# A recurrence's level products: three fp16 matmuls of split operands, or one fp32 matmul

## The chip, the core and the metric

One core of one Trainium2 chip runs the whole program. The metric is the device time of one execution in microseconds (us); the kernel before took 3277.73 us (median of 3 runs, 3277.06 to 3282.74). A core has five engines that run side by side, each taking its own instructions in order: TensorE (PE; its weight loads are listed as PEld), VectorE (DVE), ScalarE (ACT), GpSimd (POOL) and SyncE (SP), which issues DMAs.

## What is computed

Two transformer blocks over 2048 tokens of width 1024. The change lies in the second, in its recurrence (HGRN2), four heads of 128 channels each over 16 meta tokens and 2048 tokens:

```
def hgrn2(q, f_raw, i, lb):
    # f = lb + (1-lb) sigmoid(f_raw), S_t = diag(f_t) S_{t-1} + (1-f_t) i_t^T, o_t = S_t^T q_t
    ...
    diff = bcum[:, :, :, None, :] - bcum[:, :, None, :, :]
    decay = jnp.exp(jnp.where(tri[:, :, None], diff, -jnp.inf))
    scores = jnp.sum(qc[:, :, :, None, :] * decay * kc[:, :, None, :, :], axis=-1)
    o_intra = jnp.einsum('bhts,bhsv->bhtv', scores, vc)
    new_state = (jnp.exp(b_last[:, :, 0, :])[..., None] * state
                 + jnp.einsum('bhsk,bhsv->bhkv', kc * jnp.exp(b_last - bcum), vc))
    return new_state, o_inter + o_intra
```

The same block has a sparse attention of 8 heads (a latent of 128, 256 selected keys), then a gated output projection and a layer norm.

## The kernel before, in words

The program runs in phases: projections and attention of the first block, projections of the second, a selection of keys, and then `phase_dsa`, in which three things are woven together: the second block's attention (4 groups of 512 queries times 8 heads, 32 steps), the output projection (`out2`, `norm2`), and the recurrence (`Hgrn`, the class at line 1811).

An attention step computes scores in `pst` (lines 2101 to 2113), takes their exponential on ScalarE (line 747), splits it in two fp16 parts `phi` (ScalarE, line 749) and `plo` (mostly GpSimd, line 753), and multiplies by the values with three fp16 matmuls (lines 777 to 779). Beside it the next head's score maxima are found: a matmul into `p` (line 2052) and a masked maximum on VectorE (line 2058), collected in `mu`, written by line 764 to 766 into `zrow`, and turned by a matmul (line 769).

`Hgrn.chunk(t)` (line 1870) works off 256 tokens, t = 0 to 7, as eight blocks (four heads, two halves of 128 tokens). A block's 128 by 128 matrix of decayed scores `Ts` is built by seven levels m = 1, 2, 4 ... 64: at a level, the queries in the upper half of each group of 2m tokens meet the keys of its lower half. `kq` (fp32, k in its first half, q in its second) holds keys and queries with the decay up to the group's border multiplied in. A level does this:

- ScalarE casts the needed columns of `kq` to fp16, `Xh` (line 1911); what is lost is `Xl`, a subtraction (line 1912), on GpSimd at levels 0, 2 and 4 (`XP`), on VectorE at the others. Both have two buffers (`XB`).
- TensorE makes eight products of 64 columns into `pl`, each from three fp16 matmuls: high by high, high by low, low by high (lines 1917 to 1919).
- VectorE copies `pl` under a mask into `Ts` (line 1924; line 1921 at m = 64).
- `double` (line 1838) multiplies, in place, the decay of the other half group into `kq`: k on GpSimd (`UP`), q on VectorE (line 1846), and joins two decays in `dc` (line 1847).

After the levels, `Ts` and the state give the output `o` in fp32 matmuls (lines 1935 and 1936), `update` moves the state on (lines 1855 to 1867), and the rows are normalised (lines 1942 to 1953). Line 1899 (eight fp32 matmuls with a moving operand of one column) makes the diagonal.

The order on each engine is not written by hand: the builder emits attention steps and fills them with chunks and projection tiles at given places (`CH`, `O2`), each with a priority (`PC`, `PO`), and a scheduler puts every engine's instructions in order by its own costs before the program runs. In the trace, chunk 0 to 7 lie between 2270 and 3070 us of the span. A second copy of `phase_dsa` stands in a branch that these inputs don't take.

Of the kernel before, what the change touches and what calls it, by code (L numbers as in the profile page):

```python
# [13 lines left out]
F16 = mybir.dt.float16  # L14
# [3 lines left out]
ALU = mybir.AluOpType  # L18
# [16 lines left out]
LATE = -800  # L35

KSC = 2.0 ** 14
XP = (0, 2, 4)
FB, XB, OT = 1, 2, "o"
UP = (0, 1, 2, 3, 4, 5, 6)  # L40
UQ = ()

# [44 lines left out]
def ap(t, off, pat):  # L87
    return bass.AP(tensor=t.tensor, offset=t.offset + off, ap=[list(p) for p in pat])
# [1722 lines left out]
class Hgrn:  # L1811
# [58 lines left out]
    def chunk(self, t):  # L1870

        K, sp, lp = self.K, self.sp, self.lp
        nc = K.nc
# [31 lines left out]
        d, o = fT.rearrange("p h t -> p (h t)"), 0  # L1905
        for li, m in enumerate(LEVELS):

            X = ap(kq, 0, [list(kq.ap[0]), [2 * m, 512 // m], [1024 + m, 2], [1, m]])
            hi, lo = (sp.tile([128, 8, 128], F16, name=n, bufs=XB) for n in ("Xh", "Xl"))
            h3, l3 = (x.rearrange("p h (n a m) -> p (h n) a m", a=2, m=m) for x in (hi, lo))  # L1910
            nc.scalar.copy(h3, X)
            (nc.gpsimd if li in XP else nc.vector).tensor_tensor(l3, X, h3, op=ALU.subtract)
            p = self.py.tile([128, 8, 64], F32, name="pl", tag="y")
            M = 64 if m == 64 else 128
            for h in range(8):
                qv = [x[:, h].rearrange("p (n a m) -> p n a m", a=2, m=m)[:, :, 1] for x in (hi, lo)]
                nc.tensor.matmul(p[:M, h], lhsT=hi[:, h, :M], rhs=qv[0], start=True, stop=False)
                nc.tensor.matmul(p[:M, h], lhsT=hi[:, h, :M], rhs=qv[1], start=False, stop=False)
                nc.tensor.matmul(p[:M, h], lhsT=lo[:, h, :M], rhs=qv[0], start=False, stop=True)
            if m == 64:  # L1920
                nc.vector.tensor_copy(Ts[:64, :, 64:], p[:64])
            else:
                d4 = lambda x: x.rearrange("p h (n m) -> p h n m", m=m)
                nc.vector.copy_predicated(Ts.rearrange("p h (n a m) -> p h n a m", a=2, m=m)[:, :, :, 1],
                                          d4(self.mk[:, li, None, :].to_broadcast([128, 8, 64])), d4(p))
            dn = dt[:, o:o + 512 // m]
            self.double(kq, d, dn, m, 2, li)
            d, o = dn, o + 512 // m
# [403 lines left out]
```

## Time and profile before

| | |
|---|---|
| median of 3 runs | 3277.73 us (3277.06 to 3282.74) |
| the profiled execution | 3274.8 us, span 3272.7 us |
| PE busy | 2951.4 us, 90% of the span, 25152 instructions |
| PEld busy | 1846.6 us, 56%, 25152 |
| DVE busy | 2132.7 us, 65%, 5113 |
| ACT busy | 1698.7 us, 52%, 3066 |
| POOL busy | 1430.2 us, 44%, 1239 |

How to read the profile: busy time is the union of an engine's instruction records. Records of matmuls overlap (each holds its way through the array), so what a matmul costs TensorE in a row of them is the distance between starts, not the duration of a record. An fp32 matmul of the program stands in the trace as two records of MATMUL and two of LDWEIGHTS. A wait is put down to the instruction that ended it. The granted clock is a share of full speed, 2.4 GHz.

### The profile page before, as it was taken

What the parts mean: (1) busy time and instruction counts of PE and PEld (TensorE: products, weight loads), DVE (VectorE), ACT (ScalarE), POOL (GpSimd) and SP (SyncE); (2) the same over time, 40 slices, a digit from 0 to 9 for tenths busy, and PEclk for the clock granted to TensorE, in tenths of its full rate; (3) what the DMA queues carried; (4) which work ended last, traced back from release to release, by engine and by line L of the source; (5) the groups of instructions that cost most, each with busy time, mean ns of one, the idle gap of its engine ahead of it and who ended that gap; (6) DMA issues with size and microseconds to landing.
All of it is one profiled execution on the core that took longest, in us unless ns stands there. A gap on an engine that the chain in (4) does not pass through costs nothing. (4 is left out here: it accounts for less than half of the span.)

```text
span 3272.7 us, 65807 instructions
## 1 busy us (share of the span) xinstructions
PE 2951.4 (90%) x25152; PEld 1846.6 (56%) x25152; DVE 2132.7 (65%) x5113; ACT 1698.7 (52%) x3066; POOL 1430.2 (44%) x1239
## 2 busy tenths in 40 slices
PE   6899999999996999999999899898878888989997
PEld 5554444577873555544445684366655566556653
DVE  7523865566667676545598799612787678787653
ACT  4423755666566556534364574223654465555662
POOL 3311456644234555423234416411454466575652
PEclk9999999999996999999999899898778989898998
DMA  6222344432334434134334522315543533432331
GB/s 236 82 87 75 114 126 122 147 95 66 94 110 138 123 126 133 66 107 139 99 98 108 184 84 70 106 63 141 146 109 94 158 109 91 120 107 78 93 101 68
DMA packets 264431, 361.17 MB, mean 110 GB/s; under 512 B 55372, under 2 KB 185280, under 8 KB 262952
## 3 DMA queue, kind: packets, MB, share of 16 engines
q1 hardware_dynamic: 263672, 356.84, 35.6%
q8 instruction: 199, 3.26, 0.4%
q14 instruction: 128, 1.05, 0.1%
q10 hardware_dynamic: 432, 0.02, 0.0%
HBM read 243.94 MB, written 112.82 MB: 109 GB/s over the span
## 5 line engine op out<-in xcount | busy, mean ns | idle before, releaser
L753 POOL TENSOR_TENSOR plo<-p,phi 128x512 f16<-128x512 f32 (+4 forms) x628 | 689.0, 1109 | 729.8 <-ACT phi L749 439.3
L749 ACT CAST phi<-p 128x512 f16<-128x512 f32 (+4 forms) x681 | 365.7, 557 | 135.3 <-PE po L779 112.0
L747 ACT ACTIVATE p<-pst,shift,dci 128x512 f32<-128x512 f32 (+4 forms) x352 | 247.2, 716 | 145.1 <-PE pst L2113 60.0
L777 PE MATMUL po<-v,phi 128*128 128x65 f16 (+1 forms) x2304 | 300.7, 197 | 10.5 <-ACT phi L749 6.1
L778 PE MATMUL po<-v,phi 128*128 128x64 f16 (+1 forms) x2304 | 299.2, 198 | 0.0
L779 PE MATMUL po<-v,plo 128*128 128x65 f16 (+1 forms) x2304 | 283.1, 196 | 16.1 <-POOL plo L753 12.5
L777 PEld LDWEIGHTS <-phi 128*128 128x128 f16 (+1 forms) x2552 | 246.6, 99 | 65.1 <-issue 15.1
L2058 DVE CUSTOM_DVE_ANT_0 jk<-p,mk 128x512 bf16<-128x512 f32 (+2 forms) x320 | 193.8, 606 | 134.9 <-PE p L2052 76.6
L779 PEld LDWEIGHTS <-plo 128*128 128x128 f16 (+1 forms) x2552 | 245.7, 101 | 61.9 <-POOL plo L753 28.6
L747 ACT ACTIVATE p<-pst,shift,fci 128x512 f32<-128x512 f32 (+1 forms) x320 | 219.2, 710 | 108.5 <-PE pst L984 59.8
L963 DVE TENSOR_REDUCE mu<-p 128x1 f32<-128x512 f32 (+2 forms) x320 | 188.2, 604 | 128.2 <-PE p L959 85.6
L284 POOL TENSOR_TENSOR wlo<-wraw,whi 128x512 f16<-128x512 f32 (+3 forms) x116 | 151.2, 1320 | 238.5 <-ACT whi L283 211.6
L778 PEld LDWEIGHTS <-phi 128*128 128x128 f16 (+1 forms) x2552 | 246.6, 100 | 13.8 <-issue 2.9
L337 PE MATMUL pp<-whi,hhi 128*128 128x256 f16 (+2 forms) x824 | 234.9, 286 | 6.3 <-ACT whi L283 5.7
L339 PE MATMUL pp<-whi,hlo 128*128 128x256 f16 (+2 forms) x824 | 232.6, 285 | 5.3 <-POOL hlo L465 5.2
L338 PE MATMUL pp<-wlo,hhi 128*128 128x256 f16 (+2 forms) x824 | 234.4, 285 | 0.6 <-POOL wlo L284 0.6
L326 PE MATMUL pp<-hhi,whi 128*128 128x512 f16 (+2 forms) x496 | 190.0, 383 | 4.4 <-DVE ra L523 4.4
L328 PE MATMUL pp<-hhi,wlo 128*128 128x512 f16 (+2 forms) x496 | 190.0, 383 | 0.0
L327 PE MATMUL pp<-hlo,whi 128*128 128x512 f16 (+2 forms) x496 | 189.7, 383 | 0.0
L328 PEld LDWEIGHTS <-wlo 128*128 128x128 f16 (+2 forms) x1000 | 99.8, 100 | 123.1 <-issue 12.2
L326 PEld LDWEIGHTS <-whi 128*128 128x128 f16 (+2 forms) x1000 | 100.2, 101 | 118.7 <-issue 13.6
L327 PEld LDWEIGHTS <-whi 128*128 128x128 f16 (+2 forms) x1000 | 100.0, 101 | 114.8 <-issue 16.7
(655 smaller groups left out, 8819.5 us busy)
## 6 DMA issues: line engine op xcount, KB each, us to landing
wraw<-in_w_in_dram SPq DMA_DIRECT2D x88, 256.0 KB
d_z<-er SPq DMA_DIRECT2D x128, 128.0 KB
bT<-d_rb SPq DMA_DIRECT2D x32, 384.0 KB
wa<-in_w_ada_dram SPq DMA_DIRECT2D x8, 1024.0 KB
x<-in_x_dram SPq DMA_DIRECT2D x16, 512.0 KB
d_k<-ehi SPq DMA_DIRECT2D x32, 256.0 KB
d_q<-ehi SPq DMA_DIRECT2D x32, 256.0 KB
QA<-d_q SPq DMA_DIRECT2D x64, 128.0 KB
```

The lines of the kernel that those rows point to most:

```text
L326: nc.tensor.matmul(ps, lhsT=whi, rhs=hhi[:, kk, :], start=kk == 0, stop=False)
L327: nc.tensor.matmul(ps, lhsT=whi, rhs=hlo[:, kk, :], start=False, stop=False)
L328: nc.tensor.matmul(ps, lhsT=wlo, rhs=hhi[:, kk, :], start=False, stop=kk == KK - 1)
L337: nc.tensor.matmul(ps, lhsT=hhi[:, kk, s], rhs=whi, start=kk == 0, stop=False)
L338: nc.tensor.matmul(ps, lhsT=hhi[:, kk, s], rhs=wlo, start=False, stop=False)
L339: nc.tensor.matmul(ps, lhsT=hlo[:, kk, s], rhs=whi, start=False, stop=kk == KK - 1)
L747: nc.scalar.activation(p, s, AF.Exp, scale=ci[:m], bias=K.shift[:m])
L749: nc.scalar.copy(hi, p)
L753: e.tensor_tensor(lo, p, hi, op=ALU.subtract)
L777: nc.tensor.matmul(o, lhsT=hi, rhs=v[:, :65], start=first, stop=False, **kw)
L778: nc.tensor.matmul(o[:, 1:65], lhsT=hi, rhs=v[:, 65:129], start=False, stop=False, **kw)
L779: nc.tensor.matmul(o, lhsT=lo, rhs=v[:, :65], start=False, stop=last, **kw)
```

## The change

The split goes. At a level, each of the eight blocks gets one matmul whose operands are slices of `kq` itself, in fp32; cast, subtraction, `Xh`, `Xl` and their two constants are gone.

```diff
-XP = (0, 2, 4)
-FB, XB, OT = 1, 2, "o"
+FB, OT = 1, "o"
...
-            X = ap(kq, 0, [list(kq.ap[0]), [2 * m, 512 // m], [1024 + m, 2], [1, m]])
-            hi, lo = (sp.tile([128, 8, 128], F16, name=n, bufs=XB) for n in ("Xh", "Xl"))
-            h3, l3 = (x.rearrange("p h (n a m) -> p (h n) a m", a=2, m=m) for x in (hi, lo))
-            nc.scalar.copy(h3, X)
-            (nc.gpsimd if li in XP else nc.vector).tensor_tensor(l3, X, h3, op=ALU.subtract)
             p = self.py.tile([128, 8, 64], F32, name="pl", tag="y")
             M = 64 if m == 64 else 128
             for h in range(8):
-                qv = [x[:, h].rearrange("p (n a m) -> p n a m", a=2, m=m)[:, :, 1] for x in (hi, lo)]
-                nc.tensor.matmul(p[:M, h], lhsT=hi[:, h, :M], rhs=qv[0], start=True, stop=False)
-                nc.tensor.matmul(p[:M, h], lhsT=hi[:, h, :M], rhs=qv[1], start=False, stop=False)
-                nc.tensor.matmul(p[:M, h], lhsT=lo[:, h, :M], rhs=qv[0], start=False, stop=True)
+                c = slice(h % 2 * 128, h % 2 * 128 + 128)
+                qv = q[:, h // 2, c].rearrange("p (n a m) -> p n a m", a=2, m=m)[:, :, 1]
+                nc.tensor.matmul(p[:M, h], lhsT=k[:, h // 2, c.start:c.start + M], rhs=qv, start=True, stop=True)
```

The scheduler orders the program anew. Up to the first chunk's diagonal every engine's order is the same as before; from there on it differs throughout. Lines of the changed kernel are lower by 7 behind the products (line 1846 is 1845, line 1924 is 1917, line 2052 is 2045, line 2111 is 2104, line 2177 is 2170).

TensorE, fourth chunk, level m = 8, before. `pl` is the level's result, `p_...` are score maxima's, `pst` the attention's scores, `po` its output, `QA` and `KA` its queries and keys:

```order
L2052 MATMUL p_34384<-KA,QA 128x512
L1917 LDWEIGHTS Xh
L1917 MATMUL pl<-Xh 128x64
L779 LDWEIGHTS plo
L779 MATMUL po<-v,plo 128x65
...
L777 MATMUL po<-v,phi 128x65
L778 LDWEIGHTS phi
L778 MATMUL po<-v,phi 128x64
L1918 LDWEIGHTS Xh
L1918 MATMUL pl<-Xl,Xh 128x64
L1919 LDWEIGHTS Xl
L1919 MATMUL pl<-Xh,Xl 128x64
```

The level's first matmul needs only `Xh` and runs early; the other 23 follow when `Xl` is there, with attention between. The same chunk now, levels m = 8, 16 and 32:

```order
L1912 MATMUL pl<-kq 128x64 x8
L2045 LDWEIGHTS QA
L2045 MATMUL p_33487<-KA,QA 128x512
L2045 LDWEIGHTS QA
L2045 MATMUL p_33518<-KA,QA 128x512
L2048 LDWEIGHTS bTb
L2048 MATMUL p_33518<-jb,bTb 128x128
L2048 LDWEIGHTS bTb
L2048 MATMUL p_33518<-jb,bTb 128x128
L1912 MATMUL pl<-kq 128x64 x16
L768 LDWEIGHTS zrow_124
```

Eight matmuls make a level; between m = 8 and m = 16 stand four matmuls of the score maxima, between m = 16 and m = 32 none.

VectorE, the same chunk, levels m = 4 and 8, before (`xr` is the output projection's, `jk` and `mu` the score maxima's):

```order
L1912 TENSOR_TENSOR Xl<-kq,Xh 128x1024
L2058 ISA jk,mu<-p_34384,mk_31257 128x512
L2058 ISA mu 128x1
L1846 TENSOR_TENSOR kq<-kq,dc 128x64x8
L2058 ISA jk,mu<-p_34413,mk_31257 128x256
L2058 ISA mu 128x1
L1924 COPY_PREDICATED Ts<-lmk,pl 128x64x8
```

And now, levels m = 8 and 16:

```order
L1917 COPY_PREDICATED Ts<-lmk,pl 128x64x8
L1845 TENSOR_TENSOR kq<-kq,dc 128x64x8
L2170 SCALAR_TENSOR_TENSOR xr<-xr,r_32844,lbb 128x1024
L2051 ISA jk,mu<-p_33487,mk_30981 128x512
L2051 ISA mu 128x1
...
L1917 COPY_PREDICATED Ts<-lmk,pl 128x32x16
L1845 TENSOR_TENSOR kq<-kq,dc 128x32x16
```

Before, the doubling of q stood behind its subtraction and ahead of the copy into `Ts`; now the copy, which reads `pl` and so waits for TensorE, stands ahead of the doubling.

## Rows read from the trace of the kernel before

**Rows 1.** The view of busy time by stretch: the stage with the recurrence (2270 to 3070 us of the span), its first part and the rest, and the tail behind it. Columns: stretch, its length, then for each engine busy us and the number of records, then the granted TensorE clock, the DMA share and GB/s.

```profile
core 0: us, PE busy (x) PEld busy (x) DVE busy (x) ACT busy (x) POOL busy (x), PEclk, DMA share, GB/s
2270.00:3070.00 800.00, 697.45 (x7658) 472.21 (x7657) 612.46 (x1244) 455.36 (x745) 474.84 (x373) 0.88 0.39 112
3070.00:3272.00 202.00, 178.66 (x1708) 103.39 (x1706) 103.88 (x227) 99.27 (x168) 88.67 (x81) 0.96 0.30 93
```

**Rows 2.** The view of waits, TensorE's matmuls, 2270 to 3070 us: who waited for whom, us in total, times, the longest us.

```profile
PE p L2052 <- DVE mu L2058: 43.5, 18, 7.7
PE p L769 <- DVE zrow L766: 17.7, 10, 3.6
PE p L2064 <- DMA KA<-d_k: 7.5, 6, 1.7
PE y L1147 <- DVE oTlo L346: 6.7, 1, 6.7
PE po L779 <- POOL plo L753: 5.9, 6, 1.8
PE pl L1917 <- ACT Xh L1911: 3.9, 2, 2.2
PE p L2052 <- DVE mu L2069: 3.4, 5, 1.8
PE pl L1918 <- DVE Xl L1912: 2.7, 6, 0.6
PE y L1899 <- DVE xr L2151: 1.9, 1, 1.9
PE p L769 <- DVE dd L1901: 1.7, 1, 1.7
PE pst L2086 <- ACT QA L770: 1.2, 3, 0.7
```

**Rows 3.** The chain of waits that ended last, its part from 2880 to 3070 us, shares by engine, tile and line.

```profile
by line: issue 11.7%; DVE jk L2058 8.4%; DVE o L1953 7.2%; PE p L2052 5.3%; POOL plo L753 4.5%; PE pst L2101 4.2%; PE pst L2113 4.0%; PE pst L2102 3.8%; PE y L1147 2.5%; PE y L1935 2.5%; ACT p L747 2.5%; PE y L1936 2.4%; PE po L779 2.3%; PE
```

**Rows 4.** Groups of instructions by line and form, 2270 to 3070 us: line, engine, operation, names, shapes, count, then busy us and mean ns of one, then the engine's idle time before them and what ended it.

```profile
L753 POOL TENSOR_TENSOR plo<-p,phi 128x512 f16<-128x512 f32 x152 | 194.6, 1292 | 106.1 <-ACT phi L749 66.9 <-PE p L2052 16.3 <-PE po L779 15.8
L2058 DVE CUSTOM_DVE_ANT_0 jk<-p,mk 128x512 bf16<-128x512 f32 x184 | 126.2, 686 | 69.8 <-PE p L2052 52.1 <-PE p L2055 12.2
L1846 POOL TENSOR_TENSOR kq<-kq,dc 128x512 f32<-128x512 f32 x48 | 65.9, 1373 | 48.5 <-DVE Xl L1912 28.8 <-DVE zrow L766 11.5 <-DVE r L786 8.0
L1911 ACT CAST Xh<-kq 128x1024 f16<-128x1024 f32 x56 | 63.0, 1125 | 61.8 <-PE pl L1919 17.3 <-DVE kq L1846 16.9 <-POOL kq L1846 8.1
L1846 DVE TENSOR_TENSOR kq<-kq,dc 128x512 f32<-128x512 f32 x48 | 58.8, 1224 | 2.8 <-POOL Xl L1912 2.6
L1912 POOL TENSOR_TENSOR Xl<-kq,Xh 128x1024 f16<-128x1024 f32 x24 | 54.1, 2255 | 13.4 <-ACT Xh L1911 12.7 <-PE po L779 0.8
L1924 DVE COPY_PREDICATED Ts<-lmk,pl 128x512 f32<-128x512 int32 x48 | 43.4, 905 | 11.2 <-PE pl L1919 7.6 <-PE po L779 3.5
L1912 DVE TENSOR_TENSOR Xl<-kq,Xh 128x1024 f16<-128x1024 f32 x32 | 41.1, 1285 | 0.5 <-ACT Xh L1911 0.5
```

**Rows 5.** The longest stall: the timelines of VectorE and of TensorE (start us, us, engine, line, operation, names, form, count, and in brackets the idle time before and what ended it), and from the view of line 1953 its durations in ns, shortest, median and longest.

```profile
2979.59 9.26 DVE L1953 SCALAR_TENSOR_TENSOR o<-o,rs,zg 128x128 f32<-128x128 f32 x8
2989.64 0.58 PE L2052 MATMUL p<-KA,QA 64*128 64x512 f16 x1 [6.68 <-DVE mu L2058]
L1953 DVE SCALAR_TENSOR_TENSOR o<-o,rs,zg x64: 335/752/3628, 2372.3 to 3077.1; 128x128 f32<-128x128 f32 x64
```

**Rows 6.** The timeline of TensorE, two levels' fp16 products in a row: the first and the last of 23 starts each, of one at the full and of one at the half clock.

```profile
3045.08 0.19 PE L1918 MATMUL pl<-Xl,Xh 128*128 128x64 f16 x1
...
3045.72 0.19 PE L1919 MATMUL pl<-Xh,Xl 128*128 128x64 f16 x1
2287.39 0.24 PE L1918 MATMUL pl<-Xl,Xh 128*128 128x64 f16 x1
...
2288.57 0.24 PE L1919 MATMUL pl<-Xh,Xl 128*128 128x64 f16 x1
```

**Rows 7.** The view of busy time by stretch for these two and for the stretches of rows 8; columns as in rows 1.

```profile
2428.00:2431.00 3.00, 3.00 (x15) 3.00 (x16) 1.06 (x5) 0.00 (x0) 0.00 (x0) 0.50 0.02 5
2438.40:2440.00 1.60, 1.60 (x17) 1.60 (x16) 1.28 (x6) 0.41 (x1) 1.19 (x2) 1.00 0.05 14
3045.00:3045.90 0.90, 0.90 (x29) 0.85 (x26) 0.90 (x3) 0.81 (x3) 0.84 (x1) 1.00 0.81 175
2287.30:2288.70 1.40, 1.40 (x26) 1.35 (x25) 1.40 (x4) 1.12 (x3) 1.40 (x2) 0.50 0.71 143
2902.40:2904.00 1.60, 1.60 (x16) 1.60 (x16) 0.52 (x1) 0.50 (x1) 1.60 (x1) 1.00 0.05 17
```

**Rows 8.** The timeline of TensorE, fp32 matmuls: eight of one moving column (two records each) and the fp16 matmul behind them; then those of 128 moving columns at full and at half clock, the first and the last start of each.

```profile
2902.22 1.92 PE L1899 MATMUL y<-ones,E 128*128 128x1 f32 x16
2904.00 0.19 PE L778 MATMUL po<-v,phi 128*128 128x64 f16 x1
2439.07 0.39 PE L1935 MATMUL y<-V,Ts 128*128 128x128 f32 x2
...
2439.74 0.39 PE L1936 MATMUL y<-state,kq 128*128 128x128 f32 x2
2428.32 0.63 PE L1936 MATMUL y<-state,kq 128*128 128x128 f32 x2
...
2430.46 0.63 PE L1935 MATMUL y<-V,Ts 128*128 128x128 f32 x2
```

**Rows 9.** The views of lines 1899 and 1917, their weight loads: count, shortest, median and longest ns.

```profile
L1899 PEld LDWEIGHTS y<-ones,E x128: 186/192/337, 2281.9 to 3001.3; 128*128 128x128 f32 x128
L1917 PEld LDWEIGHTS <-Xh x448: 95/98/291, 2284.0 to 3051.7; 128*128 128x128 f16 x128, 128*64 128x64 f16 x22
```

**Rows 10.** The views of lines 1924 and 1846 on VectorE, durations in ns as in rows 9.

```profile
L1924 DVE COPY_PREDICATED Ts<-lmk,pl x48: 686/716/1322, 2291.7 to 3048.2; 128x512 f32<-128x512 int32 x48
L1846 DVE TENSOR_TENSOR kq<-kq,dc x48: 657/1032/6007, 2295.0 to 3051.9; 128x512 f32<-128x512 f32 x48
```

**Rows 11.** The timeline of TensorE, fp16 matmuls of 512 moving columns, ten starts apart.

```profile
2899.03 0.38 PE L1146 MATMUL y<-wolo,oThi 128*128 128x512 f16 x1
...
2901.19 0.38 PE L1147 MATMUL y<-wohi,oTlo 128*128 128x512 f16 x1
```

## The prediction

> **What bounds the kernel now.** I read the stage table first, since the change touches only `Hgrn.chunk`, which runs eight times between 2270 and 3070 us of the span [rows 1]. In those 800 us TensorE has 697 us of matmul records, VectorE 612, GpSimd 475 and ScalarE 455: TensorE is the fullest engine, VectorE second, and nobody is full. The tail from 3070 us on holds no recurrence. The list of what TensorE waited for comes next [rows 2]: its eleven lines sum to 96 us, 78 of them ended by VectorE (score maxima, `zrow`, `oTlo` and others), and only 7 by the split itself (`Xh` and, among VectorE's, `Xl`). The chain of waits reaches back to 2882 us only; over its part in the stage [rows 3], issue gaps (11.7%), VectorE's maxima and normalisation (8.4 and 7.2%), GpSimd's `plo` (4.5%) and ScalarE's exponential (2.5%) make 34% that is not TensorE; the rest is mostly many small TensorE lines. So TensorE's work is on the path for somewhat over half of the stage.
>
> **What is taken away.** Per chunk and level the split was one cast on ScalarE and one subtraction, by `XP` on GpSimd for levels 0, 2, 4 and on VectorE for the other four. By the groups of rows [rows 4] the stage loses 63.0 us of ScalarE (56 casts), 41.1 us of VectorE (32) and 54.1 us of GpSimd (24). Almost all of it lies beside TensorE's work: TensorE waited 3.9 us for `Xh` and 2.7 for `Xl` [rows 2]. These 7 us go for certain. What else the lighter engines give back is their share of the 75 us in which TensorE waited for VectorE on other things. VectorE sheds 41 of 612 us, 7%, and some slowdown beside GpSimd: its longest stall of TensorE, 6.68 us at 2989.64, stands behind eight normalisations that took 9.26 us where the shortest of that line takes 0.335 us each [rows 5]. That burst is not part of the split and stays. Bounds: 0 (only bursts like this one matter) to 75 us (all of it); I take 18, a quarter, because the work behind the longest waits is kept.
>
> **What TensorE gets.** The 24 fp16 matmuls of a level start 29 ns apart at the full clock (22 steps from 3045.08 to 3045.72) and 54 ns apart at half clock (2287.39 to 2288.57) [rows 6]; the granted clock was 1.00 and 0.50 in these stretches [rows 7]. A level costs 0.70 or 1.29 us. The stage's clock was 0.88 [rows 1], so about a quarter of it ran at half clock: 0.86 us a level, 48 us for 56 levels. The new eight products have fp32 operands of 128 weight columns and 64 moving ones. That size is not in the trace, but it lies between two that are [rows 8]: eight fp32 products with one moving column fill 2902.22 to 2904.00, 0.22 us each, and those with 128 moving columns start 0.22 us apart as well (2439.07 to 2439.74, three products). Since 1 and 128 columns cost the same at full clock, 64 do too: 1.78 us a level, 100 us for 56. At half clock 128 columns take 0.43 us (2428.32 to 2430.46, five products), which I keep as an upper end for the colder quarter: another 24 us at most. The weight load explains why: fp32 loads last 192 ns at the median where fp16 loads last 98 [rows 9], two records stand for each product, and they cannot be hidden behind so short a matmul. So TensorE gets 100 - 48 = 52 us more work, although it issues a third of the instructions.
>
> The last level has only 64 weight columns; no fp32 row here has that, so I price it between 0.03 us (an fp16 product) and 0.22 us (128 columns) and take the latter, being of the same type and nearer; the low end would take off 12 us. The Trainium skill ("TensorE: Matmul & The Clock Gate", sections "LDWEIGHTS" and "Weight-path perf modes") speaks against this change: fast weight load is off for FP32, and a load lasts by its columns. By it the last level would cost half, and the added work would be 45 us instead of 52; no run here shows a 64-column fp32 load.
>
> Of the 52 us not all lengthens the stage, because some falls where TensorE waits anyway (800 - 697 = 103 us without a record). Bounds: 0 to 52; with somewhat over half of the chain TensorE's, I take 0.6, or 31 us.
>
> **The new wait.** Before, the products read copies (`Xh`, `Xl`, two buffers each), so `double` could overwrite `kq` as soon as cast and subtraction had read it, and TensorE could be up to two levels late. Now the products read `kq` itself: `double` on GpSimd (k half) and VectorE (q half) must wait for the level's last matmul, and the next level's first matmul must wait for both. TensorE stands in order, with the attention's matmuls queued behind. In the changed order the copy into `Ts`, which waits for the same matmuls, stands ahead of the q half on VectorE, so a crossing costs the two in series: by the means of the stage 0.905 + 1.224 = 2.1 us, by the medians 0.716 + 1.032 = 1.75 [rows 10]; the k half takes 1.373 beside it [rows 4]. What hides a crossing is the other matmul work that the order puts between two levels. I counted it with the spacings of [rows 6, 8] and of the 512-column ones (0.22 us, [rows 11]): 16 of the 48 crossings have less than 2.1 us, down to none at all, and their shortfalls sum to about 20 us; at 1.75 us it is 14. Should a maximum or a `plo` stand ahead of the doubling (0.69 and 1.29 us, [rows 4]), a crossing needs 3 us and the sum is about 39. If the other waits of the stage let VectorE catch up it is near 0. I take 20. Queued behind a late level are the `plo` subtractions on GpSimd and the maxima on VectorE, which TensorE needs in turn; that is what the upper end prices.
>
> **The sum.** 31 + 20 - 7 - 18 = +26 us. The profiled execution took 3274.8 us (span 3272.7), 2.9 under the median of 3277.7; 3274.8 + 26 = 3301, and on the median's basis **3304 us**, 0.8% slower. ScalarE's 63 us and GpSimd's 54 I cost at nothing beyond this: ScalarE is busy 455 of 800 us and GpSimd 475.
>
> **The rivals.**
> - *Faster: VectorE and GpSimd set the pace.* The waits ended by VectorE vanish (-75), the split's too (-7), all the new products lie on the path (+52) and the crossings cost 14 us: -16, or 3262 us, and down to -30 if the crossings are hidden. For it: VectorE ends nearly all of TensorE's waits [rows 2], and it is slow just when GpSimd runs [rows 5]. Against: the longest waits come from work that stays. The mechanism is that a GpSimd operation holds up VectorE's, so that the 24 subtractions of 2.26 us on GpSimd cost VectorE time too, and VectorE would shed up to 95 us rather than 41. The Trainium skill ("SBUF — State Buffer", section "SBUF: two separate sides") states an exclusive lock on a shared port pair for just such pairs; the burst of [rows 5] agrees in kind, but not in proof. The point at which it decides: relief above 65 us. Chance 0.20.
> - *No change: the products fill TensorE's waits.* Of the 103 us without a record the 52 take half, and 20 of new waits replace 25 of old ones: within 6 us of 3278. For it: attention's matmuls are issued in a fixed order, and a fuller TensorE arrives later at the maxima that it now waits for. Against: the waits stand at a few places, the new products at 56 others. Chance 0.13.
> - *Much slower: the crossings become a ring.* All 52 on the path, 39 of crossings, -7: +84, or 3362 us. For it: four engines wait in order for each other, at the two levels of the fourth chunk that stand back to back with nothing between. Against: most crossings have 2.1 us and more of cover. Chance 0.15.
> - That the change doesn't do what it says is excluded by the order: 8 products a level, no cast, no subtraction.
>
> **How the numbers follow.** The forecast (+7 to +65) has 0.52. A measurement of this kernel tells 0.2%, some 6.5 us, from no change. Slower by more: 0.52 + 0.15 = 0.67; within: 0.13; faster: 0.20. The range runs from 3262, which takes in no change and the rival on the other side as far as its own value, to 3352 (52 + 39 - 7 - 10 = +74: all the products on the path, the dear crossings and little relief); it leaves out the ring's far end and the deeper gains, some 0.2 together.
>
> **What would show it.** In the profile after: eight pairs of `pl<-kq` records a level, the pairs starting 0.22 us apart (0.43 would be the half clock; 0.06, two fp16 spacings, would mean that the loads are hidden after all and that the products cost nothing more); no `Xh`, `Xl`; waits "PE pl <- DVE kq" or "POOL kq" and "POOL kq <- PE pl" summing to 15 to 40 us; VectorE busy some 550 to 570 us in the stage; the time up to 2270 us unchanged, and the tail after the last chunk as long as before. The forecast fails if the waits of TensorE for VectorE's maxima fall by more than half, or if the stage's length does not follow TensorE's work.

## The result, and the profile after

The changed kernel takes **3326.4 us** (median of 6 runs, 3313.5 to 3332.9) beside 3277.4 us of the kernel before (6 runs on the same chip): a ratio of 1.0145, 95% interval 1.0121 to 1.0169, some 48 us more. The forecast was 3304 us with a range of 3262 to 3352. The sign and the range held; the middle was 22 us too low. The profiled execution took 3320.1 us (span 3318.4).

Where the time went shows in the view of busy time by stretch, which answers to [rows 1] (columns as there; the second row runs from the first to the last product of a level):

```profile
2270.00:3070.00 800.00, 746.76 (x6682) 526.98 (x6682) 484.00 (x1132) 373.18 (x636) 379.74 (x326) 0.84 0.38 107
2276.00:3087.00 811.00, 756.46 (x6793) 533.84 (x6791) 489.41 (x1142) 377.29 (x644) 385.06 (x331) 0.84 0.38 107
3116.00:3318.00 202.00, 175.02 (x1694) 102.33 (x1692) 99.16 (x222) 98.09 (x167) 87.11 (x79) 0.96 0.28 87
```

The same stretch of the kernel before, first to last product:

```profile
2284.00:3052.00 768.00, 666.08 (x7325) 448.63 (x7324) 592.99 (x1192) 431.64 (x708) 456.24 (x359) 0.88 0.39 113
```

The products begin at 2276 us instead of 2284, and the last 202 us are as full of TensorE work (175 us) as the tail of [rows 1] (179): most of the 46 us between the two profiled executions lies between them, where the stretch grew from 768 to 811 us. What stands behind the last product took 231 us instead of 221. TensorE is 90 us fuller there, VectorE 104 emptier, ScalarE 54 and GpSimd 71. And the granted clock fell from 0.88 to 0.84. It has two levels, 0.5 and 1.0, so a mean tells the time at half clock: 2 x (1 - 0.88) x 768 = 184 us before, 2 x (1 - 0.84) x 811 = 260 us after (the means have two digits, so these are good to some 8 us).

The products themselves, in the timeline of TensorE (start us, us, line, form, count): two whole levels with 128 weight columns, then two with 64, one of each at half and at full clock.

```profile
2312.31 3.66 PE L1912 MATMUL pl<-kq 128*128 128x64 f32 x16
2630.51 1.90 PE L1912 MATMUL pl<-kq 128*128 128x64 f32 x16
2411.47 1.97 PE L1912 MATMUL pl<-kq 128*64 128x64 f32 x16
2968.81 1.15 PE L1912 MATMUL pl<-kq 128*64 128x64 f32 x16
```

The clock in these four stretches, in the same order (busy time by stretch; the clock is the third number from the end):

```profile
2312.31:2315.90 3.59, 3.59 (x23) 3.59 (x21) 0.58 (x4) 0.58 (x3) 1.05 (x2) 0.50 0.84 157
2630.51:2632.40 1.89, 1.89 (x18) 1.82 (x17) 0.00 (x0) 0.11 (x1) 1.15 (x1) 1.00 0.58 218
2411.47:2413.40 1.93, 1.93 (x18) 1.78 (x16) 1.79 (x10) 0.38 (x1) 0.00 (x0) 0.50 0.97 134
2968.81:2969.90 1.09, 1.09 (x20) 1.02 (x17) 0.00 (x0) 1.05 (x3) 0.48 (x1) 1.00 0.00 0
```

Sixteen records make a level of eight products, each in two passes. The full-clock level of 1.90 us is 1.78 plus the drain of the last record, as forecast from [rows 8]; at half clock it is 3.66. TensorE's busy time on the level's tile `pl` in the stretch from first to last product (busy us, records, clock, DMA share, GB/s) sums this up, after and before:

```profile
2276.00:3087.00 811.00, 142.82 (x896) 0.84 0.38 107
```

```profile
2284.00:3052.00 768.00, 68.37 (x1344) 0.88 0.39 113
```

So the products take 74 us more of TensorE, not 52. All at full clock they would be 48 x 1.90 + 8 x 1.15 = 100 us, all at half clock 48 x 3.66 + 8 x 1.97 = 191: 142.8 lies nearly half way, whereas the stretch as a whole was at half clock for a third of its length. Counted in the trace, 78 of the 143 us (55%) were at half clock, and 369 of the 896 records wholly; before, 23 of 68 us. The products meet the half clock more often than the work around them.

The waits of TensorE, 2270 to 3116 us, which answer to [rows 2]:

```profile
PE y L1144 <- DVE oTlo L345: 11.7, 5, 4.2
PE p L2045 <- DVE mu L2051: 10.9, 5, 5.5
PE pl L1912 <- DVE kq L1845: 7.2, 6, 2.7
PE pl L1912 <- DVE mx L2067: 5.0, 4, 2.6
...
PE p L768 <- DVE zrow L765: 2.0, 3, 1.3
```

The waits for maxima (`mu` of line 2051) fell from 43.5 to 10.9 us and those for `zrow` from 17.7 to 2.0. New are the crossings: 7.2 us for the q half (`kq`). The view of line 1912 has the rest of them, at the weight loads and on the other side (us, times):

```profile
  POOL kq L1845: 10.2, 9
  DVE kq L1845: 7.2, 6
...
who waited for it (us, times):
  POOL kq L1845: 86.0, 38
  DVE Ts L1917: 82.9, 34
```

TensorE's matmuls and weight loads wait 17 us at 15 places for the doubling. On the other side GpSimd waits 86 us for TensorE ahead of the k half, and VectorE 83 us ahead of the copy into `Ts`: these two engines now stand ready at most levels, which is what an engine with room looks like. The chain that ended last, 2880 to 3070 us, against [rows 3]:

```profile
by line: PE pl L1912 11.5%; PE p L2045 9.1%; PE pst L2094 6.7%; DVE o L1946 6.7%; PE pst L2106 6.7%; PE pst L2095 6.0%; PE po L776 4.1%; PE y L1144 3.7%; PE y L1145 3.6%; PE po L778 3.6%; DMA KA<-d_k 3.5%; PE y L1146 3.4%; issue 3.4%; PE po
```

The maxima of line 2051, 8.4% of it before (as line 2058), are not among the lines shown any more; issue gaps went from 11.7 to 3.4%; and the products head the list, where they were not among the lines shown. By this chain TensorE bounds more of the stage than before.

Last, the row of busy time over the whole execution, to be held against the table before the change:

```profile
PE 3041.7 (92%) x24704; PEld 1933.6 (58%) x24704; DVE 2037.0 (61%) x5081; ACT 1645.3 (50%) x3010; POOL 1361.8 (41%) x1215
```

VectorE sheds 2132.7 - 2037.0 = 96 us, although the 32 instructions that went had 41 us [rows 4].

### The profile page after: what moved, and what is told of

The parts are those of the page before. It is cut to its first block, busy times and chain, and to the rows that moved or that the text cites. A ratio compares the mean times of both kernels' runs of the same rounds, so it can differ in the third digit from the quotient of the medians.

```text
span 3318.4 us, 64836 instructions
## 1 busy us (share of the span) xinstructions
PE 3041.7 (92%) x24704; PEld 1933.6 (58%) x24704; DVE 2037.0 (61%) x5081; ACT 1645.3 (50%) x3010; POOL 1361.8 (41%) x1215
## 5 line engine op out<-in xcount | busy, mean ns | idle before, releaser
L752 POOL TENSOR_TENSOR plo<-p,phi 128x512 f16<-128x512 f32 (+4 forms) x628 | 671.0, 1079 | 809.8 <-ACT phi L748 510.5
```

Source lines behind the costliest of these rows:

```text
L752: e.tensor_tensor(lo, p, hi, op=ALU.subtract)
```

## The experiments

Four prices had to be told apart: the products, the crossings between TensorE and the doubling, the relief of the other engines, and the clock. One caveat holds for all of them: the scheduler orders each kernel anew, so a difference between two runs also has another order in it. Effects below some 10 us are not read as causes here, and two predictions by addition missed by some 20 (below).

All runs in one table. "Reads kq" has crossings, "copy" has none. Times are medians, ratios against the kernel before on the same chip; the next columns are of the profiled execution, from first to last product: length, clock, the time at half clock worked out as above, TensorE's busy us on `pl`; VectorE's busy us is over the whole execution.

| run | products | subtraction | us | ratio (95%) | length | clock | half clock | `pl` | VectorE |
|---|---|---|---|---|---|---|---|---|---|
| before | 3 fp16, copy | yes | 3277 | 1 | 768 | 0.88 | 184 | 68 | 2133 |
| the change | fp32, reads kq | no | 3326 | 1.0145 (1.0121 to 1.0169) | 811 | 0.84 | 260 | 143 | 2037 |
| `e1_copy` | fp32, copy | no | 3302 | 1.0085 (1.0053 to 1.0116) | 763 | 0.88 | 183 | 139 | 2035 |
| `e2_keepsplit` | fp32, reads kq | yes | 3351 | 1.0243 (1.0202 to 1.0284) | 833 | 0.83 | 283 | 137 | 2099 |
| `e8_swap` | fp32, copy | yes | 3334 | 1.0189 (1.0148 to 1.0230) | 789 | 0.87 | 205 | 133 | 2131 |
| `e4_twice` | 6 fp16, copy | yes | 3294 | 1.0057 (1.0037 to 1.0077) | 783 | 0.91 | 141 | 127 | 2116 |
| `e3_nosub` | 3 fp16, copy | no | 3225 | 0.9854 (0.9830 to 0.9877) | 687 | 0.92 | 110 | 69 | 2055 |
| `e10_poolsub` | fp32, copy | GpSimd's | 3297 | 1.0054 (1.0033 to 1.0075) | 770 | 0.87 | 200 | 134 | 2074 |
| `e9_fill` | fp32, reads kq, 16 idle | no | 3286 | 1.0017 (0.9993 to 1.0042) | 768 | 0.90 | 154 | 171 | 2032 |
| `e11_beforefill` | 3 fp16, copy, 16 idle | yes | 3285 | 1.0024 (1.0006 to 1.0042) | 760 | 0.90 | 152 | 103 | 2121 |
| `e6_double_first` | fp32, reads kq | no | 3312 | 1.0097 (1.0060 to 1.0134) | 788 | 0.85 | 236 | 135 | 2018 |
| `e12_mixed` | fp32 and fp16, copy | GpSimd's | 3290 | 1.0034 (1.0011 to 1.0057) | 767 | 0.88 | 184 | 102 | 2092 |

In the rows with idle matmuls `pl` holds these too. A profiled execution can lie up to 20 us off its median: that of `e1_copy` was the quickest of its six (3282 us beside 3302), those of `e2_keepsplit`, `e8_swap` and `e3_nosub` the quickest of four (5 to 7 us), that of `e4_twice` the second slowest of eight (3302 beside 3294), so lengths and clocks lean to that side. The stretch from first to last product also holds more of the attention's work in some kernels than in others; where that matters, the time from 2270 us to the end is given below. Two more, `e13_mixedfill` and `e15_fill_first`, are told at the end.

The theory after the first result (A in the expectations): the products cost TensorE 74 us, much of it at half clock, and the missing subtractions give back some 40. The rivals: the crossings carry the cost (B), or the split's removal gave nothing (C).

### Products, crossings and relief, two by two

`e1_copy`: the change, with a copy between.

```diff
+            X = ap(kq, 0, [list(kq.ap[0]), [2 * m, 512 // m], [1024 + m, 2], [1, m]])
+            xf = sp.tile([128, 8, 128], F32, name="Xf", bufs=2)
+            nc.scalar.copy(xf.rearrange("p h (n a m) -> p (h n) a m", a=2, m=m), X)
...
-                nc.tensor.matmul(p[:M, h], lhsT=k[:, h // 2, c.start:c.start + M], rhs=qv, start=True, stop=True)
+                qv = xf[:, h].rearrange("p (n a m) -> p n a m", a=2, m=m)[:, :, 1]
+                nc.tensor.matmul(p[:M, h], lhsT=xf[:, h, :M], rhs=qv, start=True, stop=True)
```

> The changed kernel, but ScalarE copies the operands of each level into an fp32 tile Xf with two buffers (no rounding, no subtraction), and the fp32 products read that copy. So the doubling no longer waits for TensorE, nor the products for the doubling's end other than through the copy. Theory A (TensorE's price: the products take about 140 us in the stage instead of 67, because many of them run at half clock): the waits for kq that go, some 10 us, are about what the copy's own delay costs, and the time stays between 3310 and 3332 us. Rival B (the crossings between TensorE and the doubling are what costs, also where the trace puts the wait down to something else): 3306 us or less. Rival C (ScalarE's casts were part of what the split cost): above 3332 us, since ScalarE gets its 63 us back.

`e2_keepsplit`: the change, with cast and subtraction as before, unread.

```diff
+            nc.scalar.copy(h3, X)
+            (nc.gpsimd if li in XP else nc.vector).tensor_tensor(l3, X, h3, op=ALU.subtract)
```

> The changed kernel, but the cast and the subtraction of each level are still made, into tiles that nobody reads; the products stay fp32 and read kq. Theory A (the change was a price of about 74 us on TensorE less a relief of about 40 us from the missing subtractions): the relief goes, 3350 to 3380 us, and TensorE's waits that VectorE ends come back from about 45 us to 80 or more. Rival C (the split's removal gave nothing; the waits fell because TensorE arrives later everywhere): within 8 us of the changed kernel, 3318 to 3335 us.

`e8_swap`: both, that is the kernel before with TensorE's part alone swapped.

```diff
+            nc.scalar.copy(x3, X)
+            (nc.gpsimd if li in XP else nc.vector).tensor_tensor(l3, X, x3, op=ALU.subtract)
...
+                nc.tensor.matmul(p[:M, h], lhsT=xf[:, h, :M], rhs=qv, start=True, stop=True)
```

> The kernel before with only TensorE's part swapped: ScalarE copies the operands into an fp32 tile Xf with two buffers, GpSimd or VectorE still makes the subtraction (unread, from the fp32 copy), and the products are one fp32 matmul a block on Xf. Waits and other engines' work are those of before as nearly as it goes, so the difference to 3277 us is the price of the fp32 products alone. Theory A: 67 to 140 us of products and a lower granted clock for the rest, nearly all of it on the path: 3335 to 3365 us. By the prediction's terms (52 us of products, 0.6 of it on the path): 3300 to 3315 us. Rival B (the crossings carry the cost): 3300 us or less here, and the run that keeps the split but reads kq is slower by 30 us or more.

Measured: 3302, 3351 and 3334 us. The first lies under theory A's range, the second at its lower end, the third a microsecond under it. With the change (3326) they make a square, from which the products' price can be read once and the two others twice, by the medians:

- products alone, before to `e8_swap`: **+57 us** (62 by the ratio, its interval 48 to 75). TensorE's `pl` rose from 68 to 133, so the program grew by about nine tenths of the added 65 us. The 0.6 of the prediction was far off. (In `e8_swap` the unread `Xl` has one buffer instead of two; no subtraction is seen to wait for another.)
- crossings: 3326 - 3302 = **24 us** without the subtraction, 3351 - 3334 = **17 us** with it. Rival B was right on `e1_copy` (3306 or less), and wrong that they carry the whole cost: `e8_swap` has none and is slow, and reading `kq` adds 17, not 30. In both pairs the half clock goes with the crossings (260 against 183 us, 283 against 205), while TensorE's time without a record in the stretch hardly differs (55 against 46 us, 63 against 67).
- relief, the subtraction left out: 3334 - 3302 = **32 us** with copies, 3351 - 3326 = **25 us** with crossings. So `e2_keepsplit` came out as theory A had it (3350 to 3380), but the waits did not return with it: its largest line, for `mu`, is 18.1 us, and VectorE's lines among the first eleven sum to 45, where theory A wanted 80. The relief is real and is not the sum of the waits that vanished.

Round the square the steps add up to the measured 49 either way (57 - 32 + 24, and 57 + 17 - 25), as they must: the sum is no check of the parts. What the square does show is that crossings and relief come out within 7 us of each other on both of its sides.

### Any work on TensorE, or fp32 work

```diff
+                for _ in range(2):
+                    nc.tensor.matmul(p[:M, h], lhsT=hi[:, h, :M], rhs=qv[0], start=True, stop=False)
+                    nc.tensor.matmul(p[:M, h], lhsT=hi[:, h, :M], rhs=qv[1], start=False, stop=False)
+                    nc.tensor.matmul(p[:M, h], lhsT=lo[:, h, :M], rhs=qv[0], start=False, stop=True)
```

> The kernel before with the three fp16 products of a block computed twice, the second time over the first: six fp16 matmuls of 128 by 64 instead of three, about 134 us of products in the stage if half the clock is granted as often as before, nearly the 140 us that the fp32 products take. If what costs is any work added to TensorE at these places: the same time as the run that swaps the products alone, within 10 us, 3330 to 3360 us. If fp32 products of this size bring down the granted clock and fp16 ones do not (theory A's second half): the stage's granted clock stays at 0.87 or above, where fp32 has 0.84, and the time is 15 us or more below that run, 3305 to 3335 us.

The two views of `e4_twice`, then of `e8_swap`: TensorE on `pl`, first to last product.

```profile
2293.00:3076.00 783.00, 126.69 (x2688) 0.91 0.39 111
```

```profile
2292.00:3081.00 789.00, 133.36 (x894) 0.87 0.37 107
```

3294.5 us, 18 above the kernel before, outside both ranges on the cheap side. By busy time the two put nearly the same work on TensorE (127 and 133 us) at the same levels, yet one costs 18 us and the other 57. (The waits are not quite the same: two thirds of the fp16 products still need `Xl`, the fp32 products the copy alone.) The clock went up with the fp16 work (0.88 to 0.91) and down a little with the fp32 work (0.87): 141 against 205 us at half clock. In length the two stretches differ by 6 us only, because `e8_swap` left more of the attention for the end. From 2270 us to the end, `e4_twice` and then `e8_swap` (columns as in [rows 1]):

```profile
2270.00:3299.30 1029.30, 930.87 (x10725) 622.47 (x10723) 698.13 (x1475) 559.70 (x914) 570.17 (x453) 0.91 0.37 106
2270.00:3327.30 1057.30, 955.90 (x8934) 645.01 (x8934) 715.06 (x1483) 559.81 (x914) 566.29 (x453) 0.88 0.36 104
```

Of the 28 us between these executions 25 are TensorE's busy time (931 and 956) and 3 its idle time (98 and 101). Counted in the trace, 186 and 245 us are at half clock, and a level takes about twice its time there (1.90 and 3.66 us): these 59 us are worth some 30, which covers the difference. That fp32 products of this size leave the clock low where fp16 ones raise it is what the rows show; why is not shown.

### The relief alone, and whose it is

```diff
-            (nc.gpsimd if li in XP else nc.vector).tensor_tensor(l3, X, h3, op=ALU.subtract)
...
+                for i in range(3):
+                    nc.tensor.matmul(p[:M, h], lhsT=hi[:, h, :M], rhs=qv, start=i == 0, stop=i == 2)
```

> The kernel before without its low parts: the subtraction of each level is left out, and the three fp16 products of a block all read Xh, so TensorE's work is that of before, and the output is not the reference's. This is the relief alone: 41 us of VectorE's and 54 us of GpSimd's records less, nothing added. If the relief is what the four runs so far make of it (about 30 us, with either way of reading the operands): 3240 to 3254 us, VectorE's busy time in the stage down by some 90 us, twice what was removed there. If it was only the waits for Xl that the change took away, as the prediction's smaller terms had it: 3262 to 3275 us.

3224.9 us: **52 us less** than before, more than either theory gave. The relief was worth 25 to 32 us beside dear products and is worth 52 here. The cheap products are not the only difference: here the products no longer wait for `Xl`, while the unread subtractions of the other runs held up no product. Which of the two brings the rest is not separated. From 2270 us to the end, the kernel before and `e3_nosub`:

```profile
2270.00:3272.70 1002.70, 876.11 (x9363) 575.61 (x9361) 716.34 (x1470) 554.63 (x912) 563.51 (x453) 0.90 0.37 108
2270.00:3217.80 947.80, 859.83 (x9355) 562.61 (x9353) 636.09 (x1437) 554.43 (x910) 503.05 (x429) 0.92 0.40 114
```

TensorE's idle time fell from 127 to 88 us, and the time at half clock, counted in the trace, from 204 to 146. So less waiting went with a higher clock here. It need not: in the stretch from first to last product the kernel before has 102 us without a TensorE record at a clock of 0.88, the changed kernel 55 at 0.84.

```diff
-            (nc.gpsimd if li in XP else nc.vector).tensor_tensor(l3, X, x3, op=ALU.subtract)
+            if li in XP:
+                nc.gpsimd.tensor_tensor(l3, X, x3, op=ALU.subtract)
```

(against `e8_swap`)

> The run with the copies (fp32 products on Xf, no subtraction) with GpSimd's subtractions alone put back, unread, on levels 0, 2 and 4: 24 of them, and not one instruction more for VectorE. If GpSimd's operations hold up VectorE's (the rival that forecast a gain): VectorE's busy time in the stage rises from 483 us to 515 or more, and the time by 10 to 25 us, to 3312 to 3327. If each engine's relief works by itself: VectorE stays below 495 us, and the time is within 8 us of the run with the copies, 3294 to 3310 us.

The busy rows of `e1_copy` and of `e10_poolsub`:

```profile
PE 3019.9 (92%) x24704; PEld 1915.5 (58%) x24704; DVE 2034.9 (62%) x5081; ACT 1702.4 (52%) x3066; POOL 1362.9 (42%) x1215
```

```profile
PE 3023.4 (92%) x24704; PEld 1917.0 (58%) x24704; DVE 2073.6 (63%) x5081; ACT 1701.6 (52%) x3066; POOL 1423.7 (43%) x1239
```

Each expectation was half right. The same 5081 instructions of VectorE take 39 us longer when GpSimd makes 24 subtractions (61 us): GpSimd does hold VectorE up, as the rival that forecast a gain had it. But the time did not rise: 3297 beside 3302, within the intervals. VectorE had that room. VectorE's own 32 subtractions, `e10_poolsub` to `e8_swap`, go with 37 us of time by the medians, 44 by the ratios (1.0054 and 1.0189): by these two runs the relief is VectorE's.

The Trainium skill ("SBUF — State Buffer", section "SBUF: two separate sides") has VectorE and GpSimd take turns on a shared port pair under an exclusive lock. The 39 us agree with it; no run here separates the lock from another cause of the slowing.

### What the crossings do to the clock

```diff
+            for h in range(16):
+                nc.tensor.matmul(p[:, h % 8], lhsT=K.idh, rhs=K.idh[:, :64], start=True, stop=True)
             for h in range(8):
                 c = slice(h % 2 * 128, h % 2 * 128 + 128)
```

> The changed kernel with 16 idle fp16 matmuls (identity by identity, 128 by 64) ahead of the fp32 products of each level, into the same tile, which the products then overwrite. They wait for the tile alone, not for kq, so they stand in the crossing. They add 26 us of TensorE work at the full clock's 29 ns, and save nothing by themselves. If the price of the crossings is paid through the granted clock (the stage has 261 us at half clock where the copies have 188): half clock falls to 220 us or less, and the time does not rise, 3300 to 3326 us. If the crossing is plain waiting and the clock follows from something else: the work comes on top where it isn't hidden, 3332 to 3352 us, and half clock stays above 240 us.

From the timeline of TensorE in this run, two levels with idle work right ahead of them:

```profile
2301.67 0.46 PE L1910 MATMUL pl<-idh 128*128 128x64 f16 x5
2301.93 3.66 PE L1914 MATMUL pl<-kq 128*128 128x64 f32 x16
2850.62 0.64 PE L1910 MATMUL pl<-idh 128*128 128x64 f16 x16
2851.10 1.98 PE L1914 MATMUL pl<-kq 128*128 128x64 f32 x16
```

The same stretch of `e9_fill` by busy time, first to last product:

```profile
2287.00:3055.00 768.00, 738.38 (x7667) 532.21 (x7667) 484.79 (x1142) 377.94 (x647) 389.52 (x332) 0.90 0.39 111
```

896 matmuls that compute nothing made the changed kernel **40 us faster**: 3286 us, below both ranges and level with the kernel before by its interval. The clock rose from 0.84 to 0.90. The same two lines in the kernel before, ahead of its products:

```diff
+            for h in range(16):
+                nc.tensor.matmul(p[:, h % 8], lhsT=K.idh, rhs=K.idh[:, :64], start=True, stop=True)
             for h in range(8):
                 qv = [x[:, h].rearrange("p (n a m) -> p n a m", a=2, m=m)[:, :, 1] for x in (hi, lo)]
```

> The kernel before with the same 16 idle fp16 matmuls ahead of each level's products as in the run that filled the changed kernel. There the fill took 40 us off. If it works because the changed kernel makes TensorE wait at the crossings, it finds little to fill here, and its 26 us of work show in part: 3277 to 3295 us. If TensorE's half clock in this stage (184 us before) is worth filling whatever the operands: half clock falls below 130 us and the time to 3250 to 3270 us.

3284.8 us: there it raised the clock as well (0.88 to 0.90), but its own work ate that up, +6 us, as the first reading had it. So, by these two runs, the changed kernel had a loss through the clock that the kernel before did not have to this extent. The Trainium skill ("TensorE: Matmul & The Clock Gate", section "HAM oscillation — how this bites in real kernels") describes such a loss, there with waits for transfers: waits between bursts of matmuls let the clock fall, and the next burst begins at the low one. The rows agree in part only. Of the two fp32 levels above, both right behind idle work, one ran at full clock (1.98 us) and one at half (3.66); counted in the trace, 223 of the 896 records still ran wholly at half clock, where the change has 369. No run here shows which waits lower the clock.

From 2270 us to the end, the change and `e9_fill`:

```profile
2270.00:3318.40 1048.40, 966.03 (x8830) 659.98 (x8829) 613.53 (x1425) 496.85 (x845) 491.44 (x426) 0.87 0.36 102
2270.00:3284.00 1014.00, 956.64 (x9812) 664.98 (x9810) 612.04 (x1438) 501.96 (x856) 497.21 (x429) 0.92 0.37 107
```

The idle matmuls took 25 us out of TensorE's idle time (82 to 57) and, counted in the trace, 108 us out of the time at half clock (279 to 171), which is worth some 50; against this stands the time that they take themselves. How much of it the new order did is not separated: the fill took off more than the whole price of the crossings (17 to 24).

### Attempts at something better

`e6_double_first` moves the doubling ahead of the copy into `Ts`:

```diff
+            dn = dt[:, o:o + 512 // m]
+            self.double(kq, d, dn, m, 2, li)
+            d, o = dn, o + 512 // m
             if m == 64:
                 nc.vector.tensor_copy(Ts[:64, :, 64:], p[:64])
```

> The changed kernel with the doubling written ahead of the copy into Ts, so that on VectorE the q half no longer stands behind that copy: a crossing then takes about 1.2 us by the prediction's rows instead of 2.1. If the crossings cost some 20 us: 5 to 15 us less than the changed kernel, 3311 to 3321 us, and less half clock than 261 us. If they cost nothing much, or if the copy into Ts that now comes later is what the products' tile waits for: 3322 to 3335 us.

3312.4 us, 14 less than the change, with half clock down to 236 us: as expected if the crossing costs what the two engines do in series. The intervals of the two ratios just overlap (the change's begins at 1.0121, this one's ends at 1.0134), and the order is another, so the cause is not shown by this run alone.

`e12_mixed` uses fp32 only where VectorE had the subtraction:

```diff
+            if li in XP:
...
+                nc.gpsimd.tensor_tensor(l3, X, h3, op=ALU.subtract)
+                prod = ((hi, hi), (hi, lo), (lo, hi))
+            else:
+                nc.scalar.copy(x.rearrange("p h (n a m) -> p (h n) a m", a=2, m=m), X)
+                prod = ((x, x),)
```

> The kernel before with fp32 products on ScalarE's copies at the levels whose subtraction is VectorE's (1, 3, 5 and 6), and the split in two fp16 parts kept on GpSimd's levels (0, 2 and 4). By the runs so far: the fp32 price of about 57 us for seven levels is some 30 us for these (three whole ones and the half-wide last), and VectorE's 32 subtractions are worth the 37 us by which the run with all subtractions stands above that with GpSimd's alone. If prices and reliefs add up like that: 3260 to 3278 us. If the relief is shared by both engines' subtractions in proportion to their time (41 of 95 us): 3282 to 3300 us.

3289.7 us (1.0034): the sum by levels failed by some 20 us, and the second reading fits, that the relief is shared between the engines; a price of the products that does not add up by levels would fit as well. The first of these speaks against what `e10_poolsub` said, so whose the relief is stays open. `e13_mixedfill` puts the idle work on top:

```diff
+            for h in range(16):
+                nc.tensor.matmul(p[:, h % 8], lhsT=K.idh, rhs=K.idh[:, :64], start=True, stop=True)
             for h in range(8):
                 for i, (a, b) in enumerate(prod):
```

> The mixed kernel (fp32 on copies at VectorE's levels, fp16 parts at GpSimd's) with the 16 idle fp16 matmuls ahead of each level's products. Whether the idle work pays is the granted clock's answer: if half clock falls to 130 us or less from some 190, the time is at or below the mixed kernel's, 3245 to 3272 us; if these levels have no waits that the fill could stand in, 5 to 20 us above it.

3288.9 us (1.0043, 1.0020 to 1.0065), clock 0.91 over 763 us, 137 us at half clock: the clock rose, the time stood still. Neither expectation holds.

`e15_fill_first` joins the fill and the earlier doubling:

```diff
+            for h in range(16):
+                nc.tensor.matmul(p[:, h % 8], lhsT=K.idh, rhs=K.idh[:, :64], start=True, stop=True)
...
+            self.double(kq, d, dn, m, 2, li)
+            d, o = dn, o + 512 // m
             if m == 64:
```

> The changed kernel with both mends: the doubling ahead of the copy into Ts, and 16 idle fp16 matmuls ahead of each level's products. Alone they took 14 and 40 us off. If both act on the same waits at the crossings, the second adds little: 3278 to 3290 us. If they add up, 3262 to 3277 us, which would be level with the kernel before or better: the price of the fp32 products and the relief would then cancel.

3298.7 us (1.0079, 1.0051 to 1.0107), above both ranges and 13 us above the fill alone. The two mends do not add; one spoils the other, and with a different order in each kernel I can't say by which wait. No version that makes the whole computation beat the kernel before.

## Why the prediction came out as it did

**The products** were the term that failed. The full-clock price was right (1.78 us forecast, 1.90 with the drain), and the bound of [rows 8], that 64 moving columns cost what 128 do, holds. Two factors were wrong. The old products were priced with a quarter of them at half clock, the new ones at full clock alone, with the half clock's 24 us kept as an upper end. Priced alike, the prediction's own figures give 124 - 48 = 76 us instead of 52, and 142.8 - 68.4 = 74 were measured (both sides higher than priced, with over half of the new products' time at half clock). And "0.6 of it on the path" was read from the share of a chain that covers a quarter of the stage. The swap alone shows nine tenths, and fp16 work at the same levels three tenths (18 of 58 us, `e4_twice`): such a share is no property of the place, since it also holds what the added work does to the clock. Together +57 where +31 stood.

**The last level** was priced like a whole one against the Trainium skill's rule ("TensorE: Matmul & The Clock Gate", sections "LDWEIGHTS" and "Weight-path perf modes") that a load lasts by its columns. The times of whole levels now agree with the rule: 1.15 us for 64 columns, 1.90 for 128, and 1.97 to 3.66 at half clock. Taken alone that would have moved the sum the wrong way, by 7 us.

**The crossings** were forecast at 20 us and measured at 24 and 17. The size was right, the way only in part: the trace names 17 us of waits, in the changed kernel alone, and an idle fill that shortens no crossing takes more than all of it away. With the crossings come 70 to 80 us more at half clock in both pairs of the square, and hardly any more idle time (+9 and -4 us), so a good part seems to be paid by matmuls at half clock and not in the wait itself; why the clock is lower there is not shown.

**The relief** was forecast at 7 + 18 = 25 us and measured at 25 to 32 here, 52 where the products stayed cheap. That the sizes agree is in part luck, for it came as the losing rival described it. VectorE shed 96 us, the rival's "up to 95", and the waits for maxima fell by three quarters. The text named that very fall as the sign that the forecast fails. It was not one: time that TensorE no longer waits is not time gained when there is more work to put into it. The sign should have been the sum of waits and work.

So the sum of +26 missed +48 mainly by the products' term. The scheme of the sum, two prices less a relief, held roughly; the clock, which had no term of its own, couples its parts. "No change" and "faster" each had one part right, the relief, and lacked the dear products. The ring at +84 did not come: TensorE's time without a record fell, from 102 to 55 us in the stretch.

The smaller signs: pairs of records 0.22 us apart at full and 0.43 at half clock appeared (1.78 and 3.44 a level, before the drain); the waits named there, which take in GpSimd's for the products, sum to 103 us (7 + 10 + 86), far above the 15 to 40, and only TensorE's 17 us of them lie inside; VectorE's 484 us in 800 lie below the 550 to 570; the part behind the last product is 10 us longer.

## What to carry to other kernels

When work is added to the fullest engine, don't discount it by that engine's share of a chain or by its idle time: here 65 us of fp32 products lengthened the program by 57. Price it at both clocks, on both sides of the comparison, and ask what it does to the clock: 58 us of fp16 products at the same levels cost 18. Don't read the clock off the waits: the kernel before waited more than the changed one and had the higher clock. A wait that goes can pay more than its own length where no new work takes its place (52 us with 39 us less of idle time, `e3_nosub`), and less where some does: here TensorE's idle time fell by 44 us while the program grew by 46. In this kernel it was the wrong direction to trade a helper's work for TensorE time, however few instructions that saves.

## What was not expected of the hardware

- Nearly the same TensorE time, 127 us of fp16 and 133 us of fp32 products at the same places, came with a clock of 0.91 and 0.87, and with 18 and 57 us of time.
- 896 idle matmuls made a kernel 40 us faster (clock 0.84 to 0.90), and the same 896 in its predecessor 6 us slower (0.88 to 0.90).
- 61 us of GpSimd subtractions lengthened the same 5081 instructions of VectorE by 39 us, with no rise of the time (3302 and 3297 us).
